# The experts' LayerNorm tile by tile on VectorE, with the transposes behind each tile, in a two-layer decoder trunk

## The chip, the cores and the metric

The kernel runs on one core of a Trainium2 chip. The metric is the device time of one execution in microseconds (us); lower is better. The inputs are fp32, and one execution computes the whole two-layer trunk for 512 rows of 1024 columns.

## The reference, cut to what matters

```python
def layer_norm(x, g, b):
    mu = jnp.mean(x, -1, keepdims=True)
    var = jnp.mean(jnp.square(x - mu), -1, keepdims=True)
    return (x - mu) * lax.rsqrt(var + 1e-5) * g + b

def reference(x, ...):                      # x: (1, 512, 1024)
    for l in range(2):
        mix = even_mixer(x, ...) if l == 0 else odd_mixer(x, ...)
        x = layer_norm(ALPHA * x + mix, ln_g[l, 0], ln_b[l, 0])
        ffn = routed_moe(x, router, w_gate[l], w_up[l], w_down[l])   # 2 of 16 experts per row
        x = layer_norm(ALPHA * x + ffn, ln_g[l, 1], ln_b[l, 1])      # "the experts' LN"
    return x
```

The odd mixer begins with `x @ w_in`. The part of it that the change reaches first is the product of x with 484 of those columns (the latents and some small pieces), one product per 128 rows of x.

## The kernel before, in words

The 512 rows are four tiles of 128 rows (tiles 0 to 3), each 128 partitions by 1024 columns. Two tiles share one SBUF buffer: tiles 0 and 1 are `xr_5573` in the lists of instructions of layer 0, tiles 2 and 3 `xr_5576`. Products run in fp32 in three passes: every operand is split into a high part (ScalarE copies and rounds, L185 and L203) and a low part (VectorE subtracts, L186 and L204), and `mm3` (L197 to L200) issues high times high, low times high, high times low. A few of the subtractions of weights are put on GpSimd (Pool): one quarter of the last expert's down weights (`LOW_ON_POOL`), and the four pieces of the latent weights at the start of the odd mixer. Weights come by DMA on SyncE's (SP's) queue.

In the expert stage (`moe`), each expert gathers its at most 96 rows by an indirect DMA on Pool's queue (L1100), runs gate, up and down products, and adds its result to the rows of `yd` in DRAM by an indirect DMA with addition on Pool's queue (L1175, "the scatter"). `yd` holds the rows after the first LN, so that it ends as the sum that the experts' LN needs. The last expert (15) isn't scattered: the sum so far is fetched from `yd` into the four tiles (L1222), and expert 15's rows are added on chip. `down` (two column halves of 512) gives the product; ScalarE and VectorE make its high and low parts (L1273, L1274, tile `m`); then for each tile and half, `part` (letter p) spreads the rows onto the tile by two small products and one VectorE instruction adds them and forms the row sums (L1239). `centre` (c) makes the mean on VectorE (L1245, L1246) and the sum of squares on ScalarE (L1247); `scales` (n) makes the inverse root in ten tiny VectorE instructions (lines 217 to 231; for a single tile it takes eight); `times` (m) subtracts the mean and multiplies by g; `end` (e) multiplies by the inverse root and adds b. `times` and `end` are split by columns: 768 columns on VectorE, 256 on Pool, in `end` with a ScalarE step between. `TAIL_ORDER` (one string a layer) gives the order of these steps; the part before the slash follows the first column half. What is wrapped in `keep` stays in this order on its engine; a scheduler fits the rest in.

In layer 0 `finish` does nothing, and the odd mixer then transposes the four tiles on TensorE (`transpose_x`, L276: two groups of four 128x128 blocks a tile) and splits them into XH and XL. XL reuses the buffers of `m`, XH and XL are read by the latent products (`proj_n`, 24 matmuls of 484 columns a tile). In layer 1 `finish` writes the tile to the output by a DMA on SP's queue (L1349).

Every engine runs its own list in order; an instruction that waits holds all that stands behind it on that engine. PSUM gives the transposes two banks (`ps_t`), the latent products two (`ps_a`), the row sums three (`ps_s`).

Of the kernel before, what the change touches and what calls it, by code (L numbers as in the profile page):

```python
# [15 lines left out]
AF = mybir.ActivationFunctionType  # L16
ALU = mybir.AluOpType
# [4 lines left out]
D = 1024  # L22
S = 512
NT = 4
# [16 lines left out]

AHEAD = (2, 3, 4, 0, 1, 5, 6, 8, 9, 10, 12, 13, 7, 14, 11, 15)


LN1_DVE = (0, 0, 0, 256)
LN2_DVE = 768
LN2_POOL = 256

LOW_ON_POOL = {("d", 14): (3,), ("d", 15): (2,)}

# [2 lines left out]
EVEN_ORDER = "a0 a1 a2 a3 o0 o1"  # L53
ODD_ORDER = "d0 q0 d1 q1 R0 d2 d3 r0 r1 t1 t2 t3 c0 c1 o0 o1 c2 c3"
ROUTE_ORDER = "y0 l0 y1 l1 y2 l2 y3 l3 r02 r23 r34"
TAIL_ORDER = ("p00 p10 p20 p30 / p01 c0 p11 c1 m0 m1 n02 p21 c2 p31 c3 e0 e1 m2 m3 n24 e2 e3",
              "p00 p10 / p20 p30 p01 c0 p11 c1 p21 c2 p31 c3 m0 m1 n04 e0 m2 e1 m3 e2 e3")

def rope_tables():
# [8 lines left out]
def trunk_kernel(ctx: ExitStack, tc, x_in, even_w_in, even_b_f, even_sinks, odd_w_in,  # L68
                 odd_q_norm, odd_kv_norm, odd_w_uq, odd_w_ukv, w_o, ln_g, ln_b, router_w,
                 router_b, moe_w_gate, moe_w_up, moe_w_down, rope_cs, out):  # L70
    nc = tc.nc
# [187 lines left out]
    xr = [None] * NT  # L259
# [5 lines left out]
    def new_x(j):  # L265
        t = new_xr(j)
        xr[2 * j:2 * j + 2] = [t[:, 0, :], t[:, 1, :]]
# [3 lines left out]

    def transpose_x(i, XH, XL):
        for c in range(2):
            p = ps_t()
            for k in range(4):
                T.transpose(p[:, k * 128:(k + 1) * 128], xr[i][:, (c * 4 + k) * 128:(c * 4 + k + 1) * 128], ident)  # L276
            pv = p.rearrange("p (k t) -> p k t", k=4)
            split_to(XH.t[c][:, :, i * 128:(i + 1) * 128], XL.t[c][:, :, i * 128:(i + 1) * 128], pv)

# [552 lines left out]
    def latent_load(kh, push=False):  # L832

        w = odd_w_in[0, kh * 512:(kh + 1) * 512].rearrange("(k p) c -> p k c", p=128)
        return wload(lambda v: [(v[:, :, 0:64], w[:, :, 576:640]), (v[:, :, 64:484], w[:, :, 960:1380])], 4, 484, push)

    def odd_mixer(ahead=()):
        w = odd_w_in[0].rearrange("(k p) c -> p k c", p=128)
        wo = w_o[1]
        with tc.tile_pool(name="od", bufs=1, reuse_waits="tile") as od, tc.tile_pool(name="odw", bufs=4, reuse_waits="tile") as work:  # L840
            XH = Rows("XH")
            XL = Rows("XL")
            for i in range(NT):
                transpose_x(i, XH, XL)
            cst = od.tile([128, NT, 32], F32, name="cst")
            vc = od.tile([128, NT, 64], F32, name="vc")
            wi = od.tile([128, NT, 4], F32, name="wi")
# [29 lines left out]
            for i in range(NT):  # L877
# [15 lines left out]
                p = ps_t()  # L893
# [153 lines left out]
            return wo_src, oH, oL, 0  # L1047


    def moe(l, mo, sl, ps2, oht, x1d, yd, flag, following, finish):  # L1050
        last = NE - 1
        nload = [0]
        prev = [None]
# [164 lines left out]
        for i in range(NT):  # L1218
            if i % 2 == 0:
                new_x(i // 2)  # L1220
            with tc.issue_after(hold[0].ins):
                hold[0] = nc.sync.dma_start(xr[i], yd[i * 128:(i + 1) * 128, :])  # L1222

# [6 lines left out]
        def keep(ins):  # L1230
            return tc.keep_in_program_order(ins)
# [20 lines left out]

        def times(i):

            n = LN2_POOL
            if n:
                G.tensor_scalar(xr[i][:, 0:n], xr[i][:, 0:n], ls[:, i, 3:4], 1.0, op0=ALU.add, op1=ALU.mult)
                G.tensor_tensor(out=xr[i][:, 0:n], in0=xr[i][:, 0:n], in1=gb[:, 0:n], op=ALU.mult)
            keep(V.scalar_tensor_tensor(out=xr[i][:, n:], in0=xr[i][:, n:], scalar=ls[:, i, 3:4], in1=gb[:, n:],  # L1259
                                        op0=ALU.add, op1=ALU.mult))  # L1260

        def end(i):
            cs, vs = slice(0, D - LN2_DVE), slice(D - LN2_DVE, D)
            if cs.stop:
                A.activation(out=xr[i][:, cs], in_=xr[i][:, cs], func=AF.Copy, scale=rs_of[i])
                G.tensor_tensor(out=xr[i][:, cs], in0=xr[i][:, cs], in1=bb[:, cs], op=ALU.add)
            keep(V.scalar_tensor_tensor(out=xr[i][:, vs], in0=xr[i][:, vs], scalar=rs_of[i], in1=bb[:, vs],  # L1267
                                        op0=ALU.mult, op1=ALU.add))
            finish(i)

        h = hidden(sg, 2)
        for steps, (c, cs, o) in zip(TAIL_ORDER[l].split("/"), down(last, raw, *h)):
            A.activation(out=m2[:CAP, 0, cs], in_=o[:CAP], func=AF.Copy, scale=gl)  # L1273
            V.scalar_tensor_tensor(out=m2[:CAP, 1, cs], in0=o[:CAP], scalar=gl, in1=m2[:CAP, 0, cs].bitcast(F32),  # L1274
                                   op0=ALU.mult, op1=ALU.subtract)
            for f, *n in steps.split():
                {"p": part, "c": centre, "n": scales, "e": end, "m": times}[f](*map(int, n))


    def dense_moe(l, finish):  # L1280
# [64 lines left out]
                ln_apply(xr[i], mv[:, 0, 0:1], rs, gb, bb)  # L1345
                finish(i)

    def write_out(i):
        nc.sync.dma_start(out[0, i * 128:(i + 1) * 128, :], xr[i])  # L1349

    flags = const.tile([128, 2], F32, name="flags")

# [5 lines left out]
    yd0 = dram.tile([S, D], F32, name="yd0")  # L1358
    yd1 = dram.tile([S, D], F32, name="yd1")

    def layer(l, proj, x1d, yd, following, finish):
        with tc.tile_pool(name="mo", bufs=1, reuse_waits="tile") as mo:
            sl, ps2, oht = out_proj(l, *proj, x1d, yd, mo, True)
            moe(l, mo, sl, ps2, oht, x1d, yd, flags[:, l:l + 1], following, finish)

    early = []
    layer(0, even_mixer(), x1d0, yd0, lambda: early.extend(latent_load(kh, True) for kh in range(2)), lambda i: None)
    layer(1, odd_mixer(early), x1d1, yd1, lambda: None, write_out)
    most = const.tile([128, 1], I32, name="most")
    V.tensor_reduce(out=flags[:, 0:1], in_=flags, axis=AX.X, op=ALU.max)  # L1370
    V.tensor_copy(most, flags[:, 0:1])
# [35 lines left out]
```

## Time and profile before

| | |
|---|---|
| median of 3 runs | 1181.48 us (1177.25 to 1182.6) |
| the profiled execution | 1180.26 us, of which the span of instructions 1178.5 us |
| TensorE busy | 1093.0 us, 93% of the span |
| mean granted TensorE clock | 0.954 of full speed |
| VectorE, ScalarE, Pool busy | 79%, 65%, 23% |

The span is the time from the first to the last instruction; the execution lasts 1.76 us longer. Times of rows count from the start of the span. A busy share is a mean over stages with different limits: the two stages that the change touches are the hand-over from layer 0 to layer 1 (about 552 to 615 us) and the end (from about 1155 us).

### The profile page before, as it was taken

What the parts mean: (1) busy time and instruction counts of PE and PEld (TensorE: products, weight loads), DVE (VectorE), ACT (ScalarE), POOL (GpSimd) and SP (SyncE); (2) the same over time, 40 slices, a digit from 0 to 9 for tenths busy, and PEclk for the clock granted to TensorE, in tenths of its full rate; (3) what the DMA queues carried; (4) which work ended last, traced back from release to release, by engine and by line L of the source; (5) the groups of instructions that cost most, each with busy time, mean ns of one, the idle gap of its engine ahead of it and who ended that gap; (6) DMA issues with size and microseconds to landing.
All of it is one profiled execution on the core that took longest, in us unless ns stands there. A gap on an engine that the chain in (4) does not pass through costs nothing. (4 is left out here: it accounts for less than half of the span.)

```text
span 1178.5 us, 16701 instructions
## 1 busy us (share of the span) xinstructions
PE 1093.0 (93%) x5775; PEld 817.5 (69%) x5775; DVE 934.3 (79%) x1866; ACT 762.3 (65%) x1229; POOL 266.5 (23%) x223
## 2 busy tenths in 40 slices
PE   8999989979999999998599898999799999999982
PEld 7786767867777777776377665777677777777761
DVE  4646756597999999987766998766879999999976
ACT  4556646235888888887435744654268888888862
POOL 2001340251111141112613133003411111411023
PEclk9999999988999999999699998999789999999997
DMA  8314332779999997998512211335699999989972
GB/s 209 117 40 90 75 88 105 255 276 303 302 358 357 350 334 237 361 357 279 183 28 72 73 37 37 107 108 209 240 299 285 365 342 353 339 255 366 371 234 108
DMA packets 139613, 262.25 MB, mean 223 GB/s; under 512 B 11831, under 2 KB 28247, under 8 KB 139520
## 3 DMA queue, kind: packets, MB, share of 16 engines
q1 hardware_dynamic: 129232, 234.62, 57.9%
q0 software_dynamic: 10288, 26.48, 9.1%
q8 instruction: 47, 0.77, 0.3%
q14 instruction: 46, 0.38, 0.1%
HBM read 246.73 MB, written 22.30 MB: 228 GB/s over the span
## 5 line engine op out<-in xcount | busy, mean ns | idle before, releaser
L186 DVE TENSOR_TENSOR wl<-wraw,wh 128x1024 fp32r<-128x1024 f32 (+1 forms) x418 | 503.6, 1231 | 83.3 <-ACT wh L185 74.9
L185 ACT CAST wh<-wraw 128x1024 fp32r<-128x1024 f32 (+3 forms) x436 | 445.7, 1039 | 155.0 <-PE ps_s L200 63.8
L198 PE MATMUL ps_s<-wh,m 128*96 128x512 f32 (+1 forms) x528 | 208.3, 394 | 1.7 <-ACT m L203 1.7
L199 PE MATMUL ps_s<-wl,m 128*96 128x512 f32 (+1 forms) x528 | 206.4, 391 | 0.0
L200 PE MATMUL ps_s<-wh,m 128*96 128x512 f32 (+1 forms) x528 | 205.0, 388 | 0.4 <-DVE m L204 0.4
L200 PEld LDWEIGHTS ps_s<-wh,m 128*96 128x96 f32 x528 | 86.4, 164 | 35.7 <-DVE m L204 1.3
L198 PEld LDWEIGHTS ps_s<-wh,m 128*96 128x96 f32 x528 | 86.7, 164 | 34.8 <-ACT m L203 2.1
L199 PEld LDWEIGHTS ps_s<-wl,m 128*96 128x96 f32 x528 | 86.4, 164 | 31.9 <-issue 0.2
L198 PE MATMUL ps_a<-wh,hH 128*96 128x512 f32 x256 | 102.7, 401 | 3.8 <-ACT hH L203 3.8
L199 PE MATMUL ps_a<-wl,hH 128*96 128x512 f32 x256 | 101.8, 398 | 4.0 <-POOL wl L186 4.0
L200 PE MATMUL ps_a<-wh,hL 128*96 128x512 f32 x256 | 101.0, 394 | 1.3 <-DVE hL L204 1.3
L198 PE MATMUL ps_a<-wh,XH 128*128 128x512 f32 (+2 forms) x224 | 89.4, 399 | 4.3 <-ACT wh L185 3.2
L1100 POOL DMA_INDIRECT m<-x1d,idx x30 | 33.1, 1104 | 255.8 <-PE ps_t L1111 224.2
L200 PE MATMUL ps_a<-wh,XL 128*128 128x512 f32 (+2 forms) x224 | 88.7, 396 | 1.9 <-DVE XL L204 1.9
L1175 POOL DMA_INDIRECT yd<-m,idx x30 | 49.2, 1640 | 177.0 <-ACT m L1174 173.3
L199 PE MATMUL ps_a<-wl,XH 128*128 128x512 f32 (+2 forms) x224 | 88.8, 396 | 0.0
L199 PE MATMUL ps_a<-XL,wh 128*128 128x512 f32 x160 | 65.0, 406 | 0.0
L200 PE MATMUL ps_a<-XH,wl 128*128 128x512 f32 x160 | 64.7, 405 | 0.3 <-DVE wl L186 0.3
L198 PE MATMUL ps_a<-XH,wh 128*128 128x512 f32 x160 | 64.6, 403 | 0.0
L357 ACT ACTIVATE p<-p,nm 128x256 f32<-128x256 f32 (+3 forms) x96 | 50.6, 529 | 17.8 <-DVE nm L350 8.8
L376 ACT COPY pT<-ps_t 128x512 f32<-128x512 f32 (+2 forms) x88 | 43.4, 517 | 28.8 <-PE ps_t L373 28.0
L199 PEld LDWEIGHTS ps_a<-wl,hH 128*96 128x96 f32 x256 | 41.3, 161 | 20.5 <-POOL wl L186 5.4
(327 smaller groups left out, 1918.3 us busy)
## 6 DMA issues: line engine op xcount, KB each, us to landing
wraw<-in_moe_w_up_dram SPq DMA_DIRECT2D x64, 1024.0 KB
wraw<-in_moe_w_gate_dram SPq DMA_DIRECT2D x64, 1024.0 KB
wraw<-in_moe_w_down_dram SPq DMA_DIRECT2D x64, 1024.0 KB
wraw<-in_w_o_dram SPq DMA_DIRECT2D x6, 1024.0 KB
wraw<-in_even_w_in_dram SPq DMA_DIRECT2D x4, 1024.0 KB
x1d<-xr POOLq DMA_DIRECT2D x8, 512.0 KB
yd<-xr POOLq DMA_DIRECT2D x8, 512.0 KB
xr<-yd SPq DMA_DIRECT2D x8, 512.0 KB
```

Of the source, the lines that this page charges most:

```text
L185: first(A.copy(hv, w))
L186: first(eng.tensor_tensor(out=lv, in0=w, in1=hv.bitcast(F32), op=ALU.subtract))
L198: T.matmul(o, lh, rh, start=first, stop=False)
L199: T.matmul(o, lh, rl, start=False, stop=False)
L200: T.matmul(o, ll, rh, start=False, stop=last)
L357: A.activation(out=pt[h], in_=(pt if bias else Sp)[h], func=AF.Exp, bias=nm[:, h:h + 1], scale=(slopes[0][h] if slopes else 1.0), accum_ou ...
L376: A.copy(d_, s_)
L1100: G.indirect_dma_start(out=xg_of[e], out_offset=None, in_=x1d[:, :], in_offset=bass.IndirectOffsetOnAxis(ap=idx[:CAP, e:e + 1], axis=0), b ...
L1175: G.indirect_dma_start(out=yd[:, :], out_offset=bass.IndirectOffsetOnAxis(ap=idx[:CAP, e:e + 1], axis=0), in_=yos[e % 2], in_offset=None, ...
```

## The change

Four things change. The LN of the experts uses VectorE alone for `times` and `end`, over all 1024 columns; Pool's and ScalarE's shares go. `TAIL_ORDER` of layer 0 takes the tiles one after the other: scales, times, end, transposes (letter t, `turn_x`), where before two tiles went together and the transposes followed the whole LN. In layer 0 the four fetches of `yd` are issued on Pool's queue right after the last scatter, and no longer on SP's queue behind the latent weights. In layer 1 the last tile is finished and written out in two halves of 512 columns.

```diff
-LN2_DVE = 768
-LN2_POOL = 256
...
-TAIL_ORDER = ("p00 p10 p20 p30 / p01 c0 p11 c1 m0 m1 n02 p21 c2 p31 c3 e0 e1 m2 m3 n24 e2 e3",
+TAIL_ORDER = ("p00 p10 p20 p30 / p01 c0 p11 c1 n01 m0 e0 p21 c2 p31 c3 t0 n12 m1 e1 t1 n24 m2 e2 t2 m3 e3 t3",
               "p00 p10 / p20 p30 p01 c0 p11 c1 p21 c2 p31 c3 m0 m1 n04 e0 m2 e1 m3 e2 e3")
...
-            XH = Rows("XH")
-            XL = Rows("XL")
-            for i in range(NT):
-                transpose_x(i, XH, XL)
+            if turned:
+                XH, XL = turned
+            else:
+                XH, XL = Rows("XH"), Rows("XL")
+                for i in range(NT):
+                    transpose_x(i, XH, XL)
...
         for i in range(NT):
             if i % 2 == 0:
                 new_x(i // 2)
+            if turn:
+                G.dma_start(xr[i], yd[i * 128:(i + 1) * 128, :])
+                continue
             with tc.issue_after(hold[0].ins):
                 hold[0] = nc.sync.dma_start(xr[i], yd[i * 128:(i + 1) * 128, :])
...
         def times(i):
-            n = LN2_POOL
-            if n:
-                G.tensor_scalar(xr[i][:, 0:n], xr[i][:, 0:n], ls[:, i, 3:4], 1.0, op0=ALU.add, op1=ALU.mult)
-                G.tensor_tensor(out=xr[i][:, 0:n], in0=xr[i][:, 0:n], in1=gb[:, 0:n], op=ALU.mult)
-            keep(V.scalar_tensor_tensor(out=xr[i][:, n:], in0=xr[i][:, n:], scalar=ls[:, i, 3:4], in1=gb[:, n:],
-                                        op0=ALU.add, op1=ALU.mult))
+            keep(V.scalar_tensor_tensor(out=xr[i], in0=xr[i], scalar=ls[:, i, 3:4], in1=gb, op0=ALU.add, op1=ALU.mult))
 
         def end(i):
-            cs, vs = slice(0, D - LN2_DVE), slice(D - LN2_DVE, D)
-            if cs.stop:
-                A.activation(out=xr[i][:, cs], in_=xr[i][:, cs], func=AF.Copy, scale=rs_of[i])
-                G.tensor_tensor(out=xr[i][:, cs], in0=xr[i][:, cs], in1=bb[:, cs], op=ALU.add)
-            keep(V.scalar_tensor_tensor(out=xr[i][:, vs], in0=xr[i][:, vs], scalar=rs_of[i], in1=bb[:, vs],
-                                        op0=ALU.mult, op1=ALU.add))
-            finish(i)
+            for cs in ((slice(0, 512), slice(512, D)) if i == NT - 1 and not turn else (slice(0, D),)):
+                keep(V.scalar_tensor_tensor(out=xr[i][:, cs], in0=xr[i][:, cs], scalar=rs_of[i], in1=bb[:, cs],
+                                            op0=ALU.mult, op1=ALU.add))
+                finish(i, cs)
...
+    def turn_x(i):
+        if not turned:
+            turned.extend((Rows("XH"), Rows("XL")))
+        transpose_x(i, *turned)
```

Where the instructions stand now, at the three places that the prediction speaks of (the changed kernel's line numbers are three or four off: its L183 is L186 before, L201 is L204, L273 is L276, L195 to L197 are L198 to L200; L1258 is `times` and L1263 `end`).

Pool in layer 0, from the last scatter (`yd_140<-m_3139`); `wl<-wraw_5560` is the quarter of expert 15's down weights, the `wl` of 968 columns are the latent weights. Before, with the semaphores that each waits for:

```order
L1175 DMA yd_140<-m_3139,idx 512x1024 [waits DMASW0_49,Activation_49]
L186 TENSOR_TENSOR wl<-wraw_5560,wh 128x1024 [waits DMAHW1_49,Activation_49]
L186 TENSOR_TENSOR wl<-wraw,wh 128x968 [waits DMAHW3_49,DMAHW2_49,Activation_49]
L186 TENSOR_TENSOR wl<-wraw,wh 128x968 [waits PE_49,Activation_49]
L186 TENSOR_TENSOR wl<-wraw,wh 128x968 [waits DMAHW5_49,DMAHW4_49,Activation_49]
```

And now:

```order
L1175 DMA yd_140<-m_3139,idx 512x1024 [waits DMASW0_49,Activation_49]
L1222 DMA xr_5573<-yd_140 128x1024 [waits DMAHW6_49,DMAHW4_49,DMASW1_49]
L1222 DMA xr_5573<-yd_140 128x1024 [waits DMASW3_49]
L1222 DMA xr_5576<-yd_140 128x1024 [waits DMAHW7_49,DMAHW3_49,DMAHW1_49]
L1222 DMA xr_5576<-yd_140 128x1024 [waits DMASW5_49]
L183 TENSOR_TENSOR wl<-wraw_5560,wh 128x1024 [waits DMAHW1_49,Activation_49]
```

Four DMA issues have come between the scatter and the subtraction of expert 15's weights; the first of them waits for DMASW1, the semaphore on which the scatter's landing is counted.

VectorE in layer 0, from the last instruction of the inverse root for tiles 2 and 3 (`rs_o`); XL are the low parts behind the transposes. Before:

```order
L231 SCALAR_TENSOR_TENSOR rs_o<-rs_c,rs_r 128x2
L1267 SCALAR_TENSOR_TENSOR xr_5576<-xr_5576,rs_o,lnt 128x768 x2
L204 TENSOR_TENSOR XL_5752<-ps_t,XH_5750 128x4x128
L204 TENSOR_TENSOR XL_5753<-ps_t,XH_5751 128x4x128
L204 TENSOR_TENSOR XL_5752<-ps_t,XH_5750 128x4x128
L204 TENSOR_TENSOR XL_5753<-ps_t,XH_5751 128x4x128
```

And now:

```order
L228 SCALAR_TENSOR_TENSOR rs_o<-rs_c,rs_r 128x2
L1258 SCALAR_TENSOR_TENSOR xr_5576<-xr_5576,ls,lnt 128x1024
L1263 SCALAR_TENSOR_TENSOR xr_5576<-xr_5576,rs_o,lnt 128x1024
L201 TENSOR_TENSOR XL_5703<-ps_t,XH_5701 128x4x128
L201 TENSOR_TENSOR XL_5704<-ps_t,XH_5702 128x4x128
L1258 SCALAR_TENSOR_TENSOR xr_5576<-xr_5576,ls,lnt 128x1024
L1263 SCALAR_TENSOR_TENSOR xr_5576<-xr_5576,rs_o,lnt 128x1024
```

Tile 2's two low parts now stand between tile 2's LN and tile 3's, so tile 3's LN comes behind them.

TensorE in layer 0 at the end of tile 1's latent product (`lat` is a finished latent tile that is transposed for the next step):

```order
L197 MATMUL ps_a<-wh,XL_5704 128x484
L273 MATMUL ps_t<-ident,xr_5576 128x128 x16
L895 MATMUL ps_t<-ident,lat 128x128 x3
L195 MATMUL ps_a<-wh,XH_5701 128x484
L196 MATMUL ps_a<-wl,XH_5701 128x484
```

Before, the transposes of tiles 2 and 3 stood inside tile 0's latent product, in groups of eight and four with products between; now the sixteen stand together behind tile 1's product, and the three transposes of tile 0's `lat` stand before the first product of tile 2.

## Rows read from the trace of the kernel before

**Rows 1.** The page's first part: busy us, share of the span, instructions of each engine.

```profile
PE 1093.0 (93%) x5775; PEld 817.5 (69%) x5775; DVE 934.3 (79%) x1866; ACT 762.3 (65%) x1229; POOL 266.5 (23%) x223
```

**Rows 2.** The view by stretches, around the hand-over: length, then busy us and instructions of each engine, the granted TensorE clock, DMA share and GB/s.

```profile
core 0: us, PE busy (x) PEld busy (x) DVE busy (x) ACT busy (x) POOL busy (x), PEclk, DMA share, GB/s
...
547.70:549.60 1.90, 0.02 (x1) 0.00 (x0) 1.58 (x1) 1.23 (x2) 1.85 (x1) 1.00 0.56 216
...
550.40:553.60 3.20, 3.20 (x15) 2.90 (x13) 1.83 (x3) 1.62 (x2) 1.12 (x1) 0.50 0.25 81
...
567.10:587.30 20.20, 8.15 (x21) 4.17 (x20) 16.98 (x46) 9.06 (x15) 14.28 (x13) 0.59 0.61 195
587.30:591.00 3.70, 3.66 (x13) 3.30 (x14) 2.24 (x10) 1.17 (x2) 0.00 (x0) 0.50 0.00 0
591.00:615.00 24.00, 23.50 (x117) 19.01 (x117) 15.20 (x67) 8.33 (x31) 4.33 (x5) 0.99 0.06 12
```

**Rows 3.** The timeline of Pool at the hand-over: start us, length us, line, what, and in brackets the idle time before it and what ended that.

```profile
552.48 1.70 POOL L1175 DMA_INDIRECT yd<-m,idx  x1 [2.92 <-ACT m L1174]
558.54 2.42 POOL L186 TENSOR_TENSOR wl<-wraw,wh 128x1024 fp32r<-128x1024 f32 x1 [4.37 <-ACT wh L185]
```

**Rows 4.** The timeline of SP's queue, and of the DMA view of 560 to 561 us the line of Pool's queue (q0: packets, MB, share of 16 engines); in the DMA view of 561 to 562 us q0 has no line.

```profile
562.30 2.27 SPq L1222 DMA_DIRECT2D xr<-yd  x4
...
q0 software_dynamic: 2, 0.00, 2.9%
```

**Rows 5.** The groups of instructions that touch `xr`, those of Pool's two kinds of DMA issue: count, lengths in ns (least, median, most), first and last start.

```profile
L591 POOL DMA_DIRECT2D x1d<-xr x8: 594/594/742, 231.9 to 851.3; - x8
L594 POOL DMA_DIRECT2D yd<-xr x8: 531/531/536, 232.6 to 851.9; - x8
```

**Rows 6.** The timeline of TensorE and, for the ends of tile 0's and tile 1's latent products, the ScalarE copies behind them.

```profile
561.06 0.42 PE L199 MATMUL ps_a<-wl,hH 128*96 128x512 f32 x1
...
562.37 0.48 PE L200 MATMUL ps_a<-wh,hL 128*96 128x512 f32 x1 [0.64 <-DVE hL L204]
...
566.51 0.39 PE L199 MATMUL ps_a<-wl,hH 128*96 128x512 f32 x1
566.74 0.40 PE L200 MATMUL ps_a<-wh,hL 128*96 128x512 f32 x1
...
580.89 0.69 PE L276 MATMUL ps_t<-ident,xr 128*128 128x128 f32 x2 [5.38 <-POOL xr L1266]
582.39 1.54 PE L276 MATMUL ps_t<-ident,xr 128*128 128x128 f32 x6 [0.81 <-DVE xr L1267]
...
593.40 1.09 PE L276 MATMUL ps_t<-ident,xr 128*128 128x128 f32 x8
...
615.07 0.39 PE L198 MATMUL ps_a<-XH,wh 128*128 128x512 f32 x1
...
597.32 0.22 ACT L879 COPY vc<-ps_a 128x64 f32<-128x64 f32 x1
...
603.37 0.21 ACT L879 COPY vc<-ps_a 128x64 f32<-128x64 f32 x1 [5.14 <-PE ps_a L200]
```

**Rows 7.** The timeline of VectorE and one row of ScalarE (the square of a tile), in the same columns.

```profile
546.11 1.23 DVE L186 TENSOR_TENSOR wl<-wraw,wh 128x1024 fp32r<-128x1024 f32 x1 [2.52 <-ACT wh L185]
...
559.66 2.38 DVE L186 TENSOR_TENSOR wl<-wraw,wh 128x1024 fp32r<-128x1024 f32 x1 [0.59 <-ACT wh L185]
...
568.36 0.75 DVE L1274 SCALAR_TENSOR_TENSOR m<-ps_a,gslot,m 96x512 fp32r<-96x512 f32 x1 [3.31 <-ACT m L1273]
569.02 0.68 DVE L1239 CUSTOM_DVE_ANT_0 xr<-ps_s,xr 128x512 f32<-128x512 f32 x1
...
573.47 0.75 DVE L1239 CUSTOM_DVE_ANT_0 xr<-ps_s,xr,ls 128x512 f32<-128x512 f32 x1 [0.58 <-PE ps_s L1238]
...
579.27 0.16 DVE L231 SCALAR_TENSOR_TENSOR rs_o<-rs_c,rs_r 128x2 f32<-128x2 f32 x1
...
586.56 0.68 DVE L204 TENSOR_TENSOR XL<-ps_t,XH 128x512 fp32r<-128x512 f32 x1
...
600.11 0.48 DVE L888 SCALAR_TENSOR_TENSOR lat<-ps_a,rs_o,qg 128x256 f32<-128x256 f32 x1
...
572.87 1.15 ACT L1247 ACTIVATE sq<-xr,ls 128x1024 f32<-128x1024 f32 x1 [3.66 <-DVE ls L1245]
```

**Rows 8.** Two 512 KB writes that Pool issued in layer 1, and when its queue q0 moved packets: the timeline of Pool, then the queue lines of the DMA views of 841 to 846 us (q0 has no line there) and of 846 to 848 us.

```profile
841.23 0.59 POOL L591 DMA_DIRECT2D x1d<-xr  x1 [0.30 <-POOL xr L256]
...
q1 hardware_dynamic: 781, 1.57, 97.0%
...
q0 software_dynamic: 102, 0.42, 51.2%
```

**Rows 9.** The timeline of VectorE at the end of the kernel, and of SP's queue.

```profile
1159.94 2.61 DVE L1259 SCALAR_TENSOR_TENSOR xr<-xr,ls,lnt 128x768 f32<-128x768 f32 x2
1162.47 0.16 DVE L222 TENSOR_SCALAR rs_v<-ls 128x4 f32<-128x4 f32 x1
...
1165.41 1.02 DVE L1267 SCALAR_TENSOR_TENSOR xr<-xr,rs_o,lnt 128x768 f32<-128x768 f32 x1
...
1170.54 2.40 DVE L1267 SCALAR_TENSOR_TENSOR xr<-xr,rs_o,lnt 128x768 f32<-128x768 f32 x2
...
1167.03 6.44 SPq L1349 DMA_DIRECT2D out_dram<-xr  x4
```

More of the change, by code (lines that the diff above doesn't have):

```diff
@@ L835, in latent_load, with odd_mixer @@
         return wload(lambda v: [(v[:, :, 0:64], w[:, :, 576:640]), (v[:, :, 64:484], w[:, :, 960:1380])], 4, 484, push)
-    def odd_mixer(ahead=()):
+    def odd_mixer(ahead=(), turned=None):
         w = odd_w_in[0].rearrange("(k p) c -> p k c", p=128)
@@ L1047, in odd_mixer, with moe @@
             return wo_src, oH, oL, 0
-    def moe(l, mo, sl, ps2, oht, x1d, yd, flag, following, finish):
+    def moe(l, mo, sl, ps2, oht, x1d, yd, flag, following, finish, turn):
         last = NE - 1
@@ L1276, in moe @@
             for f, *n in steps.split():
-                {"p": part, "c": centre, "n": scales, "e": end, "m": times}[f](*map(int, n))
+                {"p": part, "c": centre, "n": scales, "e": end, "m": times, "t": turn}[f](*map(int, n))
     def dense_moe(l, finish):
@@ L1346, in dense_moe, with write_out @@
                 finish(i)
-    def write_out(i):
-        nc.sync.dma_start(out[0, i * 128:(i + 1) * 128, :], xr[i])
+    def write_out(i, cs=slice(0, D)):
+        nc.sync.dma_start(out[0, i * 128:(i + 1) * 128, cs], xr[i][:, cs])
     flags = const.tile([128, 2], F32, name="flags")
@@ L1359, in trunk_kernel, with layer @@
     yd1 = dram.tile([S, D], F32, name="yd1")
-    def layer(l, proj, x1d, yd, following, finish):
+    def layer(l, proj, x1d, yd, following, finish, turn=None):
         with tc.tile_pool(name="mo", bufs=1, reuse_waits="tile") as mo:
             sl, ps2, oht = out_proj(l, *proj, x1d, yd, mo, True)
[L1364 to L1368, printed above, removed]
+            moe(l, mo, sl, ps2, oht, x1d, yd, flags[:, l:l + 1], following, finish, turn)
+    early, turned = [], []
+    def turn_x(i):
+        if not turned:
+            turned.extend((Rows("XH"), Rows("XL")))
+        transpose_x(i, *turned)
+    layer(0, even_mixer(), x1d0, yd0, lambda: early.extend(latent_load(kh, True) for kh in range(2)),
+          lambda i, cs: None, turn_x)
+    layer(1, odd_mixer(early, turned), x1d1, yd1, lambda: None, write_out)
     most = const.tile([128, 1], I32, name="most")
```

## The prediction

> **What bounds the kernel now.** I read the page's busy shares first. TensorE has 93% of the span [rows 1], so the change can only pay or cost where TensorE waits. The view by stretches finds such a place at the hand-over between the layers: of the 20.2 us from 567.1 to 587.3 TensorE is busy for 8.15, at a granted clock of 0.59 of full speed, and from 591 it is full again at 0.99 [rows 2]. The timelines of the engines then say who is late. Expert 15's second column half ends on TensorE at 566.74 + 0.40 = 567.1 [rows 6]; the rows of `yd` are on chip by 569.02 at the latest, where VectorE adds to tile 0 without a wait [rows 7]; and TensorE's first transposes wait 5.38 us for the LN, from Pool's side [rows 6]. So on both sides of the LN a chain runs through several engines. The end of layer 0's debt is the end of the latent products: 603.37 for tile 1 (the copy behind it) and 615.07 + 0.39 for tile 3 [rows 6]. From there on the two kernels issue the same list up to the end, so what is late at that point stays late. At the other end of the kernel, the LN on VectorE and the last output DMA set the time [rows 9].
>
> **The change, part by part.** First VectorE's own work. A 128x1024 subtraction at 546.11 takes 1.23 us [rows 7]. `times` over 768 columns, beside Pool's share, takes 2.61 / 2 = 1.31 [rows 9]. So the full width on VectorE alone costs no more than three quarters beside Pool: I count 1.2 for each `times` and `end`. The rows say why: the same subtraction takes 2.38 at 559.66 [rows 7], while Pool subtracts from 558.54 to 560.96 [rows 3]; 1.30 of it lies before Pool's end. The Trainium skill has a rule for this ("SBUF — State Buffer", section "SBUF: two separate sides"): VectorE with two SBUF inputs and a GpSimd instruction that reads SBUF take one port pair in turn, and the loser waits out the whole instruction. The trace agrees (1.30 + 1.23 = 2.53 against 2.38); by that rule alone the LN without Pool would gain, and this is the head start below.
>
> *Pool's queue.* The four fetches now stand right behind the last scatter (issued 552.48, 1.70 us [rows 3]), and the first waits for its landing. When does it land? Pool's queue still moves 2 packets in 560 to 561 and none in 561 to 562, and SP's first fetch of the same rows, which waits for the same, starts at 562.30 [rows 4]; I take 561.6. Four issues of 0.53 to 0.59 [rows 5] hold Pool to 563.9. Then comes the quarter of expert 15's weights, 2.42, which before ended at 560.96 [rows 3]: now 566.3, or 5.3 late. The latent weights behind it have slack: TensorE needs them after 580.
>
> *TensorE until the LN.* The first column half doesn't need this quarter. The second half has 11 products behind it, 0.23 apart at full clock [rows 6] and 0.43 at half clock, which a wait of about 2 us brings on (after the 1.9 us hole at 547.7, 3.2 us at 0.50 followed [rows 2]). 566.3 + 11 products, partly slow, is 571.2 in place of 567.1: +4.1. Part of this was slack. VectorE was idle for 3.31 before the second half's `m` at 568.36 [rows 7], and now adds the first half's parts meanwhile. Tile 1's second sum, which ended at 573.47 + 0.68 = 574.15 [rows 7], ends at 575.3: +1.1.
>
> *The LN of tile 0.* The square (1.15 [rows 7] and 0.2 around it), eight root steps of 0.2 (the ten end with 0.16 each [rows 7]) and two full-width steps of 1.2 bring `e0` to 580.0. The eight transposes end at 581.3; before, they ended at 582.39 + 1.54 = 583.9 [rows 6]. Before, the low parts then stood behind the LN of tiles 2 and 3 and came at 586.56 [rows 7]; now they stand behind two additions only: 583.5. Tile 0's latent product ends at about 590 in place of 597.3, and tile 1's, one tile of 603.37 − 597.32 = 6.05 later and with its transposes ahead, at 596.9 in place of 603.4 [rows 6]: a head start of 6.4 us.
>
> *Where it goes again.* Before, tiles 2 and 3 were transposed inside tile 0's product (593.40 [rows 6]); now behind tile 1's, 16 transposes, 2.2. VectorE, in its order, does the root of tiles 2 and 3 (10 × 0.2) only behind tile 1's low parts at 592.5, then `m2`, `e2` (597), then XL of tile 2, which needs tile 2's transposes, and only then `m3`, `e3`: 598.2 + two low parts + 2.4 = 602.1. TensorE stands before tile 3's transposes for 4.0. Behind them the transposes of tile 0's `lat` wait for VectorE's L888 (0.48 a piece [rows 7], four pieces), which stands behind `e3`, a root of 1.6 and tile 3's low parts: 3.4 more. After such holes the clock is at half for about 3 us [rows 2], 1.6 lost. The sum: −6.4 + 2.2 + 4.0 + 3.4 + 1.6 = +4.8. The same walk through before's list with the same durations comes out some tenths late against its trace, so I take **+4.5**.
>
> *The rows on Pool's queue.* This is the term that no row measures. I assume SP's pace: first tile at 567.2, then 1.3 apart, the last at 571.1. For two 512 KB writes that Pool issued at 841.23 and after, its queue moved nothing until 846 while SP's queue filled the DMA engines at 97%, then 0.42 MB in 2 us [rows 8]. So a start 5 us after the issue, as there, puts the four tiles at 568.2 to 574, and walking the list with that gives another +1.5 to +2.8; no wait on Pool at all leaves the boundary at +1.6; rows up to 576 give +9. By the Trainium skill ("DMA: Bandwidth & Descriptors", section "Anatomy of one DMA — SWDGE (gpsimd) path") such a transfer takes 2.0 us plus its bytes at 436 GB/s, 3.2 us here, an estimate; the walk would then end 0.3 earlier. Rows 8 don't agree with it where the engines are full. Bounds of the boundary: +1.6 to +9. As nearest row I keep SP's own fetch, since SP's queue has then nothing behind its latent weights.
>
> *The end.* VectorE from 1159.94: `m0`, `m1` in 2.45; the root, 1162.47 to 1165.41 = 2.94 beside other work, now 2.0; five full steps of 1.2; two halves of 0.68 and 0.62 (512 columns, as the additions at 569.02 [rows 7]). Together 1159.94 + 2.45 + 2.0 + 6.0 + 1.3 = 1171.7 against 1170.54 + 2.40 = 1172.9 [rows 9]: −1.3. The last DMA carries half the bytes and SP's issues, which ran from 1167.03 to 1173.47, come earlier: up to −2.2. I take **−2.0**.
>
> Edits at nothing: ScalarE's and Pool's missing shares, since neither is waited for in their place; SP's queue without the fetches, since its next loads are for weights used after 620.
>
> The sum is +4.5 − 2.0 = +2.5 on the profiled execution's 1180.26 (span 1178.5 and 1.76 outside): 1182.8. That execution is 1.22 below the median of 1181.48, so for a median I say **1184.0**. Bounds −0.4 to +7 from the terms: 1181.1 to 1188.5.
>
> **The rivals.** *Rows land late on Pool's queue (slower).* For it: [rows 8], and Pool writes the descriptors while VectorE is working. Against: the queue of SP is empty by then. It decides from the point at which tile 3's rows land after about 572, since VectorE's additions then wait and all behind them; each microsecond costs one. At 576 the boundary is +9: 1181.5 + 9 − 2 = 1188.5.
>
> *The head start is kept (faster).* If the holes of 4.0 and 3.4 and their 1.6 of clock don't come, because tile 3's LN finds room earlier than I think, the boundary is 4.5 − 9.0 = −4.5, and the time 1181.5 − 4.5 − 2 = 1175.0. Against: VectorE's list is in order, and `m3` stands behind XL of tile 2, as the order shows.
>
> *Pool's wait doesn't happen as told.* If the scatter's semaphore comes well before 561.6, so that the quarter of the weights isn't late, the boundary is +1.6 and the time 1181.1: no change. Against: SP's own fetch at 562.30.
>
> **How the numbers follow.** The forecast has a chance of 0.60, own range 1180.5 to 1187. The late rows have 0.25, the kept head start 0.10, the harmless wait 0.05. A change under 0.5% (5.9 us) is about what a measurement of this kernel can't tell from none; the limits are 1175.6 and 1187.4. Slower: 0.05 of the forecast and 0.19 of the late rows, 0.24. Faster: 0.08 of the kept head start. The rest, 0.68, is within. The range from 1176 to 1190 leaves out the upper part of the late rows and most of the kept head start, about 0.15 together.
>
> **What would show it.** In Pool's timeline: the first fetch issue waits until about 561.6 and expert 15's subtraction ends at about 566.3. TensorE then waits about 2 us for Pool's `wl`. Tile 0's first transpose comes at about 580. Tile 1's latent product ends at about 597. Then tile 3's transposes wait about 4 us for `xr` of L1263, and three transposes of `lat` some 3.4 more; the last latent product ends near 620. At the end, the last output issue starts near 1171.7. The forecast is wrong if the additions on VectorE wait for `xr` from Pool's queue beyond 572, if TensorE doesn't wait behind tile 1's product, or if the stretch between 620 and 1155 differs in length from before's, which I take as equal.

## The result and the profile after

The changed kernel takes 1187.59 us (median of 9 runs, 1180.54 to 1194.56); the kernel before, with the runs made beside it, 1179.91 (9 runs, 1175.61 to 1182.6). The ratio is 1.007 with a 95% interval of 1.0041 to 1.0099: slower by 0.4 to 1.0%. The profiled execution took 1185.83 us, its span is 1183.9.

The page's first part, against [rows 1], already says that TensorE did no more work, only in a longer span:

```profile
PE 1093.7 (92%) x5775; PEld 816.5 (69%) x5775; DVE 933.6 (79%) x1873; ACT 758.9 (64%) x1221; POOL 250.0 (21%) x203
```

Where the span grew, the view by stretches shows. These are the columns of [rows 2], cut at the hand-over's own events: the last scatter is issued at 550.86, Pool's fetches at 557.44, expert 15's second column half ends on TensorE at 572.04, the first transposes begin at 581.29, and the last latent product ends at about 621.3.

```profile
core 0: us, PE busy (x) PEld busy (x) DVE busy (x) ACT busy (x) POOL busy (x), PEclk, DMA share, GB/s
557.44:562.18 4.74, 1.93 (x9) 1.04 (x8) 0.04 (x2) 1.64 (x3) 4.73 (x6) 1.00 0.91 293
562.18:567.60 5.42, 3.75 (x11) 2.13 (x11) 5.42 (x3) 0.84 (x1) 4.33 (x2) 0.66 0.98 357
567.60:572.04 4.44, 3.78 (x8) 2.16 (x8) 2.53 (x8) 1.00 (x1) 2.19 (x1) 0.50 1.15 283
572.04:581.29 9.25, 4.16 (x10) 2.37 (x9) 6.50 (x20) 4.06 (x6) 4.12 (x5) 0.50 0.46 141
581.29:598.00 16.71, 15.83 (x65) 12.76 (x66) 11.83 (x34) 4.40 (x8) 0.00 (x0) 0.80 0.00 0
598.00:608.00 10.00, 3.74 (x21) 3.09 (x20) 7.92 (x29) 3.87 (x16) 0.00 (x0) 0.67 0.00 1
608.00:621.30 13.30, 13.30 (x58) 11.00 (x58) 6.18 (x35) 3.50 (x13) 0.00 (x0) 0.86 0.00 1
```

VectorE's column in the second row is the one to look at: 5.42 of 5.42 us busy with 3 instructions. Its timeline names them; the start is the first number, the length the second, and the bracket tells the idle time before and what ended it.

```profile
562.16 0.75 DVE L1270 SCALAR_TENSOR_TENSOR m<-ps_a,gslot,m 96x512 fp32r<-96x512 f32 x1 [4.71 <-ACT m L1269]
562.83 4.77 DVE L183 TENSOR_TENSOR wl<-wraw,wh 128x1024 fp32r<-128x1024 f32 x1
567.52 0.68 DVE L1242 CUSTOM_DVE_ANT_0 xr<-ps_s,xr 128x512 f32<-128x512 f32 x1
...
572.80 0.75 DVE L1270 SCALAR_TENSOR_TENSOR m<-ps_a,gslot,m 96x512 fp32r<-96x512 f32 x1 [2.58 <-ACT m L1269]
```

Two things are new about the subtraction of the other quarter of expert 15's weights. The first is its place. Before, it stood ahead of the first half's `m` in VectorE's list and started at 559.66 [rows 7], 7.2 us after the last scatter's issue; `m` came behind it:

```profile
564.29 0.75 DVE L1274 SCALAR_TENSOR_TENSOR m<-ps_a,gslot,m 96x512 fp32r<-96x512 f32 x1 [1.98 <-ACT m L1273]
```

Now it stands behind this `m`, for which VectorE waits 4.71 us, and starts 12.0 us after the scatter's issue, although ScalarE's last copy of expert 15's weights ended at 556.85. The second is its length: 4.77 us, where it took 2.38 before and 1.23 alone [rows 7]. Pool's timeline shows what runs beside it:

```profile
550.86 1.70 POOL L1175 DMA_INDIRECT yd<-m,idx  x1 [2.47 <-ACT m L1174]
557.44 2.26 POOL L1222 DMA_DIRECT2D xr<-yd  x4 [4.89 <-DMA yd<-m,idx]
559.69 6.82 POOL L183 TENSOR_TENSOR wl<-wraw,wh 128x1024 fp32r<-128x1024 f32 x3
```

Against [rows 3]: the four fetches wait for the scatter, and behind them three subtractions (Pool's quarter of expert 15 and two pieces of the latent weights) stand back to back until 566.51. VectorE's instruction ends at 567.60, 1.09 us after the last of them. TensorE's timeline is the other half; its products for the row sums at 568.26 wait 2.33 us for VectorE's additions, which stand behind the subtraction, and the last six products of the second half come after them:

```profile
562.18 1.75 PE L1241 MATMUL ps_s<-m,oht 96*128 96x512 f32 x6 [2.81 <-ACT m L1269]
...
568.26 1.22 PE L1241 MATMUL ps_s<-m,oht 96*128 96x512 f32 x2 [2.33 <-DVE ls L1242]
...
571.41 0.63 PE L197 MATMUL ps_a<-wh,hL 128*96 128x512 f32 x1
572.82 4.15 PE L1241 MATMUL ps_s<-m,oht 96*128 96x512 f32 x8 [0.78 <-ACT m L1269]
581.29 1.94 PE L273 MATMUL ps_t<-ident,xr 128*128 128x128 f32 x8 [4.32 <-DVE xr L1263]
...
603.16 1.94 PE L273 MATMUL ps_t<-ident,xr 128*128 128x128 f32 x8 [4.17 <-DVE rs_v L219]
607.19 0.88 PE L895 MATMUL ps_t<-ident,lat 128*128 128x128 f32 x3 [2.09 <-DVE lat L888]
...
621.13 0.39 PE L195 MATMUL ps_a<-XH,wh 128*128 128x512 f32 x1
```

The last row, the first product behind the latent ones, is the one that stood at 615.07 in [rows 6]. It is 6.06 us later, but this execution issued its last scatter 1.6 us earlier than the one before (550.86 against 552.48), so the hand-over is better counted from the scatter. From there, in the two profiles: the second half ends at +14.7 before and +21.2 now, the first transposes begin at +28.4 and +30.4, the last latent product ends at +62.8 and +70.4. A second profile of the changed kernel (below) gives +20.8, +29.3 and +70.5.

The end of the kernel, from VectorE's and SP's timelines:

```profile
1166.73 2.47 DVE L1258 SCALAR_TENSOR_TENSOR xr<-xr,ls,lnt 128x1024 f32<-128x1024 f32 x2
...
1170.92 1.28 DVE L1263 SCALAR_TENSOR_TENSOR xr<-xr,rs_o,lnt 128x1024 f32<-128x1024 f32 x1
...
1175.71 2.60 DVE L1263 SCALAR_TENSOR_TENSOR xr<-xr,rs_o,lnt 128x1024 f32<-128x1024 f32 x3
```

```profile
1172.23 6.44 SPq L1345 DMA_DIRECT2D out_dram<-xr  x5
```

From the first `times` to VectorE's last instruction it is 1178.31 − 1166.73 = 11.6 us, 13.0 in [rows 9]; from there to the end of the span 5.6, and 1178.5 − 1172.94 = 5.6 before. So the end gains 1.4 and the hand-over loses 7.6: +6.2, against +7.7 in the medians and +5.6 between the two profiled executions.

### The profile page after: what moved, and what is told of

Its sections match the earlier page's. It is cut to its first block, busy times and chain, and to the rows that moved or that the text cites. A ratio compares the mean times of both kernels' runs of the same rounds, so it can differ in the third digit from the quotient of the medians.

```text
span 1183.9 us, 16659 instructions
## 1 busy us (share of the span) xinstructions
PE 1093.7 (92%) x5775; PEld 816.5 (69%) x5775; DVE 933.6 (79%) x1873; ACT 758.9 (64%) x1221; POOL 250.0 (21%) x203
## 5 line engine op out<-in xcount | busy, mean ns | idle before, releaser
L183 DVE TENSOR_TENSOR wl<-wraw,wh 128x1024 fp32r<-128x1024 f32 (+1 forms) x418 | 504.9, 1234 | 85.5 <-ACT wh L182 76.8
L195 PE MATMUL ps_s<-wh,m 128*96 128x512 f32 (+1 forms) x528 | 208.0, 394 | 1.7 <-ACT m L200 1.7
L197 PE MATMUL ps_s<-wh,m 128*96 128x512 f32 (+1 forms) x528 | 204.7, 388 | 0.4 <-DVE m L201 0.4
L197 PEld LDWEIGHTS ps_s<-wh,m 128*96 128x96 f32 x528 | 86.0, 163 | 35.8 <-DVE m L201 1.3
L195 PEld LDWEIGHTS ps_s<-wh,m 128*96 128x96 f32 x528 | 86.3, 163 | 34.8 <-ACT m L200 2.1
L195 PE MATMUL ps_a<-wh,hH 128*96 128x512 f32 x256 | 103.6, 405 | 3.5 <-ACT hH L200 3.5
L197 PE MATMUL ps_a<-wh,hL 128*96 128x512 f32 x256 | 101.8, 398 | 0.6 <-DVE hL L201 0.6
L195 PE MATMUL ps_a<-wh,XH 128*128 128x512 f32 (+2 forms) x224 | 89.7, 401 | 3.9 <-ACT wh L182 1.9
L197 PE MATMUL ps_a<-wh,XL 128*128 128x512 f32 (+2 forms) x224 | 89.1, 398 | 1.9 <-DVE XL L201 1.9
L1175 POOL DMA_INDIRECT yd<-m,idx x30 | 52.9, 1762 | 173.5 <-ACT m L1174 172.5
L197 PE MATMUL ps_a<-XH,wl 128*128 128x512 f32 x160 | 64.7, 404 | 0.3 <-DVE wl L183 0.3
L195 PE MATMUL ps_a<-XH,wh 128*128 128x512 f32 x160 | 64.6, 404 | 0.0
L373 ACT COPY pT<-ps_t 128x512 f32<-128x512 f32 (+2 forms) x88 | 43.6, 518 | 27.5 <-PE ps_t L370 26.8
```

The source lines that it names most:

```text
L183: first(eng.tensor_tensor(out=lv, in0=w, in1=hv.bitcast(F32), op=ALU.subtract))
L195: T.matmul(o, lh, rh, start=first, stop=False)
L197: T.matmul(o, ll, rh, start=False, stop=last)
L373: A.copy(d_, s_)
L1175: G.indirect_dma_start(out=yd[:, :], out_offset=bass.IndirectOffsetOnAxis(ap=idx[:CAP, e:e + 1], axis=0), in_=yos[e % 2], in_offset=None, ...
```

## The experiments

The first theory after the result was that the fetches on Pool's queue cost (A), against the order behind tile 0 (B).

**The fetches back on SP's queue.**

```diff
-            if turn:
-                G.dma_start(xr[i], yd[i * 128:(i + 1) * 128, :])
-                continue
```

> The changed kernel with the four fetches of layer 0 back on SP's queue, behind the latent weights; all else as changed. In the changed kernel's profile expert 15's second column half ends on TensorE 21.2 us after the last scatter was issued (550.86 to 572.04), 14.7 before the change. Theory A (the fetches on Pool's queue are what costs: the quarter of expert 15's weights comes late, VectorE's own quarter then waits 3.5 us behind Pool's latent weights, the latent weights themselves land later, and the clock falls to half): the 21.2 go back to about 15 and the time to within 3 us of the kernel before, ratio 0.998 to 1.002. Theory B (the tile-by-tile order costs, by TensorE's waits of 4.17 us before tile 3's transposes and 2.09 before those of lat): these waits stay, and the ratio stays at 1.004 or more.

Ratio 1.0005 (0.9985 to 1.0025). The second half ends 13.6 us after the scatter's issue, the latent products at 66.5. A holds for the time. B's waits are there all the same, as TensorE's rows show, and the hand-over is still 3.7 us longer than before (with the fetches on Pool's queue another 3.9 come to it, 70.4); so the order costs too, about as much within the hand-over as the queue.

```profile
599.91 1.94 PE L273 MATMUL ps_t<-ident,xr 128*128 128x128 f32 x8 [4.17 <-DVE rs_v L219]
603.95 0.87 PE L895 MATMUL ps_t<-ident,lat 128*128 128x128 f32 x3 [2.09 <-DVE lat L888]
```

**The fetches on Pool's queue alone**, in the kernel before.

```diff
+            if l == 0:
+                G.dma_start(xr[i], yd[i * 128:(i + 1) * 128, :])
+                continue
             with tc.issue_after(hold[0].ins):
```

> The kernel before with one edit: the four fetches of layer 0 on Pool's queue right behind the last scatter. Theory A: the second column half ends about 20 us after the scatter's issue in place of 14.7, and the time is 4 to 7 us longer, ratio 1.003 to 1.006. Theory B: within 1.5 us of the kernel before, ratio 0.999 to 1.001.

Ratio 1.0059 (1.0027 to 1.009): this edit alone makes nearly the whole loss. The hand-over ends at +68.4, 5.6 us later than before. The second half ends at +23.1, later still than in the changed kernel, and the rows of Pool and VectorE say why: here four of Pool's subtractions stand back to back, and VectorE's waits for all of them.

```profile
563.04 9.01 POOL L186 TENSOR_TENSOR wl<-wraw,wh 128x1024 fp32r<-128x1024 f32 x4
```

```profile
563.90 0.74 DVE L1277 SCALAR_TENSOR_TENSOR m<-ps_a,gslot,m 96x512 fp32r<-96x512 f32 x1 [2.43 <-ACT m L1276]
564.56 8.57 DVE L186 TENSOR_TENSOR wl<-wraw,wh 128x1024 fp32r<-128x1024 f32 x1
```

The place is the new one here too: behind `m`, 10.1 us after the scatter's issue. It is so in all four profiles with the fetches on Pool's queue and this quarter on VectorE (9.7 to 12.0 us), and in none of the five with the fetches on SP's queue and the same split of the quarters (ahead of `m`, 6.2 to 7.7 us). So moving the fetches also moved an instruction of VectorE, which the scheduler is free to place; why it places it there isn't shown.

**Tile 3's LN ahead of tile 2's transposes**, in the changed kernel.

```diff
-... n24 m2 e2 t2 m3 e3 t3
+... n24 m2 e2 m3 e3 t2 t3
```

> The changed kernel with tile 3's LN ahead of tile 2's transposes in VectorE's order (m2 e2 m3 e3 t2 t3). Theory B: TensorE's wait before tile 3's transposes falls from 4.17 us to under 1, the last latent product ends some 2 to 3 us earlier, and the time is 2 to 3 us under the changed kernel's (ratio to before about 1.004). Theory A alone: the wait only moves to the transposes of lat (VectorE's list is full there in any case), and the time stays that of the changed kernel, ratio 1.006 to 1.007.

Ratio 1.0044 (1.0019 to 1.0068). TensorE's wait falls from 4.17 to 1.91, not under 1, and 2.68 stand before `lat`:

```profile
607.97 1.67 PE L273 MATMUL ps_t<-ident,xr 128*128 128x128 f32 x8 [1.91 <-DVE XL L201]
612.32 0.88 PE L895 MATMUL ps_t<-ident,lat 128*128 128x128 f32 x3 [2.68 <-DVE lat L888]
```

From the first transposes to the last product it is 37.5 us, 40.0 in the changed kernel: 2.5 less, as B said. But the interval of the ratio overlaps with the changed kernel's, and the hand-over as a whole, +71.0, is no shorter in this profile, since ahead of the transposes it has the longest block of all, although VectorE's start is shown ahead of Pool's:

```profile
564.53 8.96 POOL L183 TENSOR_TENSOR wl<-wraw,wh 128x1024 fp32r<-128x1024 f32 x4
```

```profile
564.45 10.14 DVE L183 TENSOR_TENSOR wl<-wraw,wh 128x1024 fp32r<-128x1024 f32 x1
```

**The changed kernel again.**

> The changed kernel once more, as it is, for a second profile of the hand-over beside the other kernels of this group. If the 3.5 us by which VectorE's quarter waits behind Pool's latent weights and ScalarE's wait for the first latent weights are the mechanism and not an accident of one execution, both show again (VectorE's subtraction over 4 us, the second half ending 20 us or more after the scatter's issue); ratio 1.004 to 1.010.

Ratio 1.0066 (1.004 to 1.0093); VectorE's subtraction takes 5.30 us. The block is no accident.

```profile
566.78 5.30 DVE L183 TENSOR_TENSOR wl<-wraw,wh 128x1024 fp32r<-128x1024 f32 x1
```

Within A two mechanisms were left: VectorE waiting out Pool's row (P), or the latent weights landing later behind the fetches, with ScalarE standing for them in front of `m` (L). For L there is a row of the changed kernel:

```profile
560.54 1.00 ACT L182 CAST wh<-wraw 128x968 fp32r<-128x968 f32 x1 [3.48 <-DMA wraw<-in_odd_w_in_dram]
561.45 0.68 ACT L1269 ACTIVATE m<-ps_a,gslot 96x512 fp32r<-96x512 f32 x1
```

**Both quarters of expert 15 on VectorE.**

```diff
-LOW_ON_POOL = {("d", 14): (3,), ("d", 15): (2,)}
+LOW_ON_POOL = {("d", 14): (3,), ("d", 15): ()}
```

> The changed kernel with both quarters of expert 15's second half subtracted on VectorE, none on Pool (Pool keeps the four fetches and the latent weights). Theory P (what costs is that VectorE's subtraction waits out Pool's subtractions, which stand back to back behind the fetches): VectorE subtracts both quarters while Pool still waits for the scatter, in 1.2 to 1.3 us each, the second half ends 14 to 16 us after the scatter's issue (21.2 in the changed kernel), and the time falls by 5 to 7 us against the changed kernel, ratio to before 0.999 to 1.002. Theory L (what costs is that the latent weights land later behind the fetches and ScalarE stands for them in front of m): ScalarE's waits for the DMA stay, the second half still ends 19 us or more after, ratio 1.004 or more.

Ratio 1.0004 (0.9976 to 1.0033), second half at +14.6, as P said. Pool has a row of three subtractions again, but VectorE's last one, which stands ahead of `m` here, is through before it begins:

```profile
559.30 1.22 DVE L183 TENSOR_TENSOR wl<-wraw,wh 128x1024 fp32r<-128x1024 f32 x1
```

```profile
558.48 2.26 POOL L1222 DMA_DIRECT2D xr<-yd  x4 [4.66 <-DMA yd<-m,idx]
561.48 6.71 POOL L183 TENSOR_TENSOR wl<-wraw,wh 128x968 fp32r<-128x968 f32 x3 [0.74 <-ACT wh L182]
```

By itself this run doesn't exclude L: the latent weights were not late here (ScalarE's copy of them waits 1.63 us for TensorE and for no DMA). But L isn't needed: in the kernel with the fetches alone moved, ScalarE's copies wait for no DMA either, and the loss is nearly the same. The kernel with VectorE alone (below) has two such waits, 2.62 and 2.55 us, and loses nothing. The copy ahead of `m` with the fetches alone moved:

```profile
561.79 1.00 ACT L185 CAST wh<-wraw 128x968 fp32r<-128x968 f32 x1 [0.71 <-PE ps_a L200]
```

What the run doesn't separate is the place of VectorE's subtraction from Pool's row: it takes both away at once. It also shows a wait that the block had covered. VectorE's additions now stand still for the rows of `yd`, by 0.77, 0.92 and 0.52 us, the last until 16.7 us after the scatter's issue:

```profile
565.97 0.69 DVE L1242 CUSTOM_DVE_ANT_0 xr<-ps_s,xr 128x512 f32<-128x512 f32 x1 [0.77 <-DMA xr<-yd]
567.59 0.69 DVE L1242 CUSTOM_DVE_ANT_0 xr<-ps_s,xr 128x512 f32<-128x512 f32 x1 [0.92 <-DMA xr<-yd]
568.81 0.69 DVE L1242 CUSTOM_DVE_ANT_0 xr<-ps_s,xr 128x512 f32<-128x512 f32 x1 [0.52 <-DMA xr<-yd]
```

**Both quarters on Pool.**

```diff
-LOW_ON_POOL = {("d", 14): (3,), ("d", 15): (2,)}
+LOW_ON_POOL = {("d", 14): (3,), ("d", 15): (2, 3)}
```

> The changed kernel with both quarters of expert 15's second half subtracted on Pool, one behind the other, behind the fetches; VectorE has none. Theory P: no engine waits for another's port, but the second quarter comes 2 x 2.27 us behind the fetches, about 4.5 us after their last issue; the second half ends 17 to 19 us after the scatter's issue, between the changed kernel's 21.2 and 14.7 before, and the ratio is 1.002 to 1.004. Theory L: as the changed kernel, ratio 1.006 or more.

Ratio 1.0016 (0.9986 to 1.0045), second half at +19.7, a little beyond what was expected, since Pool's first fetch came 8.6 us after the scatter's issue here (6.4 with both on VectorE, 6.6 in the changed kernel); VectorE's first addition waits 3.36 us for its rows, and TensorE for the additions. The time lies between the two, as P says, but its interval doesn't exclude either end.

**One root for tiles 1 to 3, and the LN ahead of the transposes**, with the fetches on SP's queue.

```diff
-... t0 n12 m1 e1 t1 n24 m2 e2 t2 m3 e3 t3
+... t0 n14 m1 e1 m2 e2 t1 m3 e3 t2 t3
```

> The changed kernel with the fetches on SP's queue and another order of layer 0's tail: one inverse root for tiles 1 to 3, and tile 2's and 3's LN ahead of the transposes of tiles 1 and 2 (n14 m1 e1 m2 e2 t1 m3 e3 t2 t3). Theory B (the order behind tile 0 costs): the transposes of tiles 2 and 3 stand inside tile 1's product again, the wait of 4.17 us before tile 3's transposes goes, those of lat wait 2 us or less, and the time is 4 to 6 us under the one with the changed order and the fetches on SP's queue (ratio 1.0005): 0.995 to 0.997 of the kernel before. Against it: VectorE is full between the roots and lat, and the wait only moves: ratio 0.999 to 1.001.

Ratio 0.997 (0.9944 to 0.9995). The wait before tile 3's transposes is gone, 2.78 us stay before those of `lat` (2 or less were expected), and the last product ends at +60.1, 6.4 us sooner than with the changed order. This is faster than both kernels.

**VectorE alone, and nothing else**, in the kernel before; run twice.

```diff
-LN2_DVE = 768
-LN2_POOL = 256
+LN2_DVE = 1024
+LN2_POOL = 0
```

> The kernel before with one edit: times and end over all 1024 columns on VectorE alone, in both layers. By the forecast's own terms the end of the kernel is 1.3 us shorter (VectorE's last instruction about 11.7 us after the first times of layer 1, 13.0 before) and the hand-over no longer; ratio 0.998 to 1.000. Rival: without Pool's quarter VectorE is the engine that TensorE waits for at the hand-over (each pair of tiles 2 x 0.3 us more), and the ratio is 1.000 to 1.002.

> The kernel with LN on VectorE alone and nothing else changed, a second time. By its trace the hand-over is as long as before (62.9 us from the scatter's issue to the end of the latent products, 62.8 before) and the end 1.4 us shorter; if that is all, the ratio is about 0.999 and the 0.995 of the first time was partly chance. If the 0.995 comes again, some 4 us come from stretches that neither theory speaks of.

Ratios 0.9953 (0.9928 to 0.9977) and 0.9963 (0.9937 to 0.9989): better than either expectation, and also faster than both kernels. The hand-over is as long as before, +62.9 and +62.2; the first transposes come 2.1 and 1.3 us later, since all eight blocks of tile 0 now wait for VectorE's `end`, where the first two waited for Pool's 256 columns alone, and less waiting follows:

```profile
583.77 1.94 PE L276 MATMUL ps_t<-ident,xr 128*128 128x128 f32 x8 [6.88 <-DVE xr L1267]
587.94 1.12 PE L276 MATMUL ps_t<-ident,xr 128*128 128x128 f32 x4 [1.23 <-DVE XL L204]
```

At the end, times to last instruction take 11.5 us in both, 1.5 less than before. The last layer's stretch from its scatter to the end of the span is 37.0 against 39.2 in the one profile of before, the stretch in between 1 us shorter; but these vary between the profiles of all kernels (in between: 521.6 to 526.8), so where the other 3 us of the gain come from stays open.

**The two repairs together.** Three kernels have the order above or its sibling, and both quarters on VectorE: with the fetches on Pool's queue, with them on SP's, and on SP's with the sibling, which has t1 ahead of m2 (t0 n14 m1 e1 t1 m2 e2 m3 e3 t2 t3).

```diff
-LOW_ON_POOL = {("d", 14): (3,), ("d", 15): (2,)}
+LOW_ON_POOL = {("d", 14): (3,), ("d", 15): ()}
...
-... t0 n12 m1 e1 t1 n24 m2 e2 t2 m3 e3 t3
+... t0 n14 m1 e1 m2 e2 t1 m3 e3 t2 t3
```

> The changed kernel, fetches on Pool's queue kept, with two repairs: both quarters of expert 15 on VectorE, and the order with one root for tiles 1 to 3 (n14 m1 e1 m2 e2 t1 m3 e3 t2 t3). Theory P: the place of the fetches is harmless once VectorE has no subtraction to do beside Pool's row; from the scatter's issue to the end of the latent products 60 to 61 us, ratio 0.995 to 0.998. Theory L: the late latent weights show once the rest is repaired, 64 us or more, ratio 0.999 to 1.002.

> The same two repairs with the fetches on SP's queue. The 2.36 us of VectorE's quarter become 1.2, and from the scatter's issue to the end of the latent products 59 to 60 us (60.1 with the quarter on Pool); ratio 0.994 to 0.997. If Pool's quarter was no hindrance, the same 60 us and 0.997.

> As h_sp_n14 with tile 1's transposes ahead of tile 2's LN (n14 m1 e1 t1 m2 e2 m3 e3 t2 t3): tile 1's low parts no longer wait for an LN step, but tile 3's transposes stand behind tile 1's whole product. Expected 60 to 62 us from scatter to the end of the latent products, 1 us more than h_sp_n14; if TensorE's place for the transposes doesn't matter, the same.

The hand-overs are 60.8, 57.6 and 59.6 us, all as short as expected or shorter. The ratios are 0.9997 (0.9973 to 1.0021), 0.9975 (0.9948 to 1.0001) and 0.9977 (0.9952 to 1.0003). With the fetches on Pool's queue the time misses its expectation, though the hand-over met it. That hand-over is 3.2 us longer than with SP's queue, and two of VectorE's additions wait in it for their rows (0.76 and 0.93 us), so theory P's word that the place of the fetches is harmless once VectorE is out of the way holds with the changed order (66.7 with both quarters on VectorE, 66.5 with the fetches on SP's queue) but not with this one. Whether the rest is a cost outside the hand-over, or the runs fell high, these intervals don't tell. The other two are as good as the order alone, and not told apart from the kernel with VectorE alone, which needs only the two constants.

## Why the prediction was right or wrong

The direction and the range held (1187.59 in 1176 to 1190). That the range held is partly luck: the forecast's own range ended at 1187, and the part above it stood for the late rows, which are not what happened. And the case that was held the likeliest, a change within 0.5%, didn't come: slower had a chance of 0.24. The forecast was +2.5 us, measured were +7.7. By its own steps:

- *VectorE alone, 1.2 for each full-width step*: right, 2.47 / 2 beside other steps and 1.28 alone. At the end −1.3 was expected of it, −1.4 came. The further gain up to −2.0 by a half-size last DMA didn't: from VectorE's last instruction to the end of the span it is 5.6 us in the changed kernel (5.2 to 6.2 over all that have the halves) and 5.4 to 5.5 in the two profiles that write the last tile whole with VectorE alone.
- *Pool's queue held until the scatter's landing*: right in kind, too long. 6.6 us after the scatter's issue the fetches went out, not 9.1, and Pool's quarter was ready at about 562, 11.1 us after the issue in place of the 13.8 that were expected.
- *TensorE until the LN, second half at 18.7 us after the scatter's issue*: this step failed. It came at 21.2, although Pool's quarter was early. The step let TensorE wait for Pool's quarter alone and gave VectorE's quarter no term, as if it stayed where it was and nothing stood in its way. That one ended 16.7 us after the scatter's issue, 9.6 before. Of these 7.2 us, 4.8 are its later start behind `m`, and 2.4 the longer wait for Pool's row, which begins 8.8 us after the scatter's issue: before, one of Pool's subtractions was in its way, now two, and with the latent weights in time four. In its old place, from 7.2 on and at 1.23 us alone, it would by these rows have been through before Pool's row began (an estimate; no run leaves it there with the fetches on Pool's queue). The prediction had read the block off [rows 7], but applied it to the LN and not to the weights in front of it, where the moved queue brings the two engines together.
- *Tile 0's first transposes at +27.5*: +30.4, 2.5 of it lost in front.
- *The waits behind tile 0*: right in sum, not in each term. 4.0 was forecast and 4.17 measured before tile 3's transposes, but 3.4 and 2.09 before those of `lat`. Half clock cost more than was taken: it lasted about 4.6 us behind the last of these waits (granted 0.51 from 607.19 to 611.80), not 3, and tile 3's eight transposes took 1.94 at half clock. So errors cancel: from the first transposes to the last latent product about 40 was forecast (580 to 620), and 40.0 and 41.2 were measured in the two profiles.
- *Half clock after a wait of about 2 us*: not each time. In the changed kernel TensorE waited 1.83 us for Pool's `wl` until 548.44, and the granted clock behind it stayed at 1.00; in the kernel before, a like wait was followed by 0.50 [rows 2].

```profile
548.44 0.48 PE L196 MATMUL ps_a<-wl,hH 128*96 128x512 f32 x1 [1.83 <-POOL wl L183]
```

- *The end of the latent products at 615.07 + 0.39*: that row is the first product behind them; the last latent product ends at 615.23, 0.2 earlier, which changes nothing.

So of the hand-over's term, taken as +4.5 and measured as +7.6, the part behind tile 0 was right in sum, and the part ahead of it was missed by 2.9 us (+27.5 against +30.4), most of it VectorE's late subtraction and what it drew after it.

The rivals. *Rows late on Pool's queue* had about the right time, 1188.5, and is not what happened: VectorE's first addition to the rows starts at 567.52, straight behind the subtraction, with no wait for a DMA, and so do its next ones. A fitting time isn't the mechanism. The rows are the next thing to be waited for, though, as the kernel with both quarters on VectorE shows. *The head start is kept*: both holes came, as the order showed. *Pool's wait is harmless*: Pool was free earlier than thought, and it was not harmless.

## What to carry to other kernels

When instructions are moved on one engine's queue, ask not only who waits for them, but beside which instruction of another engine they now run: here four DMA issues moved three or four subtractions on Pool into the way of one on VectorE. Read the other engines' lists again too: a scheduler placed VectorE's subtraction behind `m` as soon as the fetches had moved, and the prediction looked only at the engines that the edit names. Of four edits made together, one (the fetches) lost 0.6% by itself, one (the order) lost some 4 us in the hand-over, one (VectorE alone) gained 0.4 to 0.5% (the ratio of 1.0005 with the fetches back on SP's queue says that this about offsets the order), and one (the halves) did nothing that a profile shows; the gain was in two constants.

## What the runs showed of the hardware

VectorE's subtraction of two SBUF operands doesn't get a turn between Pool's back-to-back subtractions. At the hand-over it ended 1.08 to 1.10 us after the end of Pool's whole row, in each of the nine profiles in which it met one: behind one 2.36 to 2.38 us in all (before; the fetches on SP's queue), behind two 4.77 and 5.30 (the changed kernel, twice), behind four 8.57 and 10.14. Only a pause of Pool let it in. In the changed kernel the late latent weights made this pause: ScalarE's next piece of them waits 5.75 us for its DMA, until 568.77, and Pool has nothing to subtract meanwhile. The delay that theory L blamed shortened the block.

```profile
568.77 1.00 ACT L182 CAST wh<-wraw 128x968 fp32r<-128x968 f32 x1 [5.75 <-DMA wraw<-in_odd_w_in_dram]
```

The Trainium skill ("SBUF — State Buffer", section "SBUF: two separate sides") says that whoever starts first has the port pair for the whole instruction and the other blocks; the traces agree with that for one instruction (2.36 to 2.38 us beside one, 1.23 alone), and show more: for a row of them the blocked engine waited for the row.
